# Chunk states of a Mamba-2 scan as three float32r passes on split operands, placed ahead of the samples' products

## The chip, the cores and the metric

The kernel runs on one core of one Trainium2 chip. The time is the device time of one execution in microseconds (us), start to end, weights and states read from the chip's main memory. Engines are named as the profile names them: PE is TensorE (its weight loads have a row kind of their own, PEld), DVE is VectorE, ACT is ScalarE, POOL is GpSimd, SP is SyncE, which here issues most DMAs. Each engine works its own instruction queue strictly in order; semaphores tie them together.

## What is computed

One inference step of a hybrid decoder layer for 256 prompt tokens and 8 samples of 8 tokens each (T = 320 columns). The part that matters is the chunked state-space scan of 8 groups of 8 heads. The prompt is cut in two chunks of 128 tokens. For each chunk the reference forms

```
to_end = jnp.exp(la_cs[:, :, -1:] - la_cs)
chunk_states = jnp.einsum('bcsgn,bcsgr,bcsgrp->bcgrpn', bm, to_end, xd)
```

that is, with B the 128 x 128 matrix of a chunk (tokens by state) and xw = xd * to_end its weighted inputs (128 tokens by 8 heads x 64), the product of B transposed and xw. The first chunk's state feeds the second chunk's output; both together make the prompt's final state. The samples start from states read from memory (`hin`), which are multiplied with C and then updated.

## The kernel before

Nearly all work is dense layers. `dense` and `dense2` take weights in units of 128 x 1024: SP loads a unit (`raw`), ACT rounds it to float32r (`wh`, L82), DVE makes the rest (`wl` = raw - wh, L83), and PE multiplies high by high, high by low and low by high (`mm3`, L88 to L90). `raw` has 4 buffers, `wh` and `wl` 3 each, so the unit n + 3 can be cast only when PE has done with unit n.

`mixer_ssd` runs groups g = 0 to 7. A group is a list of 18 jobs: for g < 7 six columns of the next group's input projection (`xbc`, jobs 0 to 5; each ends in a convolution of three DVE instructions L443 and a SiLU on ACT, L447), eight of the output projection of the group before (`ssm_out`), four gates. After job i the list `steps[i]` of `ssd` adds the scan's pieces: step 1 `by_token` (B transposed into `bt`, the masked product `cbm`), step 2 `x_by_token` (x transposed, `xd` = x dt on DVE, L528, `xw` = xd to_end on POOL, L530) and `sample_by_token`, step 4 `off_sample` twice (L617, eight products 32 columns wide, four side by side in PE) and `states` (L576, L579), step 5 `diagonal` (L594, whose results DVE adds with L596, called y), step 6 `off_prompt` (L605) and `off_sample_out` (transposes of `ye`, L201). The norm of the group before (`group_norm`: `ry`, L167 to L172, then L699 and splits L127, L128) comes after job 1. Group 0 has a shortened list and no norm; group 7 has `gate_pool` columns in place of the projection.

Tiles of one tag share buffers, and so does PSUM: the pool `misc` has 4 buffers handed out in turn, so each of these small products waits for the reader of the fourth before it. The framework orders the instructions of each engine ahead of time, by its own estimates; the order in the queues is fixed before the run.

Of the kernel before, what the change touches and what calls it, by code (L numbers as in the profile page):

```python
# [11 lines left out]
F32 = mybir.dt.float32  # L12
F32R = mybir.dt.float32r
AF = mybir.ActivationFunctionType
ALU = mybir.AluOpType
# [9 lines left out]
T = SEQ + NB * NS  # L25
# [28 lines left out]
def bcast(ap, shape):  # L54
    return ap.broadcast_to(list(shape))


class Kernel:
# [397 lines left out]
    def ssd(self, s, g):  # L456

        nc, I, O = self.nc, self.I, self.O
        h0 = 8 * g
        hs = slice(h0, h0 + 8)  # L460
        v = {"xd": [], "xw": [], "gt": [], "hin": {}}

        def heads(ap):
            return ap.rearrange("p (h d) -> p h d", h=8)
# [27 lines left out]
        def by_token():  # L492
            Bt, Ct = v["r"]["B"], v["r"]["C"]

            bt = v["bt"] = s.tile([128, 2, 128], F32, tag="bt", name="bt")
            ps = self.misc()
            for j in range(2):
                self.transpose(ps[:, j * 128:j * 128 + 128], Bt[:, j * 128:j * 128 + 128])
            self.transpose(ps[:64, 256:384], Bt[:, SEQ:T])
            nc.scalar.copy(out=bt.rearrange("p j n -> p (j n)"), in_=ps[:, :256])  # L500
            we = v["we"] = s.tile([128, 640], F32, tag="fin", name="we")[:64]
            nc.scalar.copy(out=we[:, 512:], in_=ps[:64, 256:384])

            cbm = s.tile([128, T], F32, tag="cbm", name="cbm")
            ps = self.misc()
            for j in range(2):
                js = slice(j * 128, j * 128 + 128)
                nc.tensor.matmul(ps[:, js], lhsT=Bt[:, js], rhs=Ct[:, js], start=True, stop=True)
            nc.tensor.matmul(ps[:64, 256:320], lhsT=Bt[:, SEQ:T], rhs=Ct[:, SEQ:T], start=True, stop=True)
            nc.vector.tensor_tensor(out=cbm[:, :SEQ].rearrange("p (j t) -> p j t", j=2),  # L510
                                    in0=ps[:, :SEQ].rearrange("p (j t) -> p j t", j=2),
                                    in1=bcast(self.cst[:, C_CM:C_CM + 128].unsqueeze(1), [128, 2, 128]), op=ALU.mult)
            nc.vector.tensor_tensor(out=cbm[:64, SEQ:], in0=ps[:64, 256:320], in1=self.cst[:64, C_SM:C_SM + 64], op=ALU.mult)

            for j, e in enumerate(v["gt"]):
                n = 128 if j < 2 else 64
                nc.vector.tensor_tensor(out=e[:n], in0=e[:n], in1=bcast(cbm[:n, j * 128:j * 128 + n].unsqueeze(1), [n, 8, n]),
                                        op=ALU.mult)

        def x_by_token():  # L520
            xs = v["r"]["x"]

            for j in range(2):
                ps = self.misc()
                for c in range(4):
                    self.transpose(ps[:, c * 128:c * 128 + 128], xs[:, c, j * 128:j * 128 + 128])
                d = s.tile([128, 512], F32, tag="xd", name="xd", bufs=2)
                nc.vector.tensor_tensor(out=heads(d), in0=heads(ps), in1=bcast(self.t_dt[:, j, hs].unsqueeze(2), [128, 8, 64]), op=ALU.mult)  # L528
                w = s.tile([128, 640], F32, tag="xw", name="xw", bufs=2)[:, :512]
                nc.gpsimd.tensor_tensor(out=heads(w), in0=heads(d), in1=bcast(self.t_end[:, j, hs].unsqueeze(2), [128, 8, 64]), op=ALU.mult)  # L530
                v["xd"].append(d)
                v["xw"].append(w)

        def sample_by_token():
            xs = v["r"]["x"]
# [17 lines left out]
        def rows_in(q):  # L553

            t = v["rw", q] = s.tile([128, 640], F32, tag="xw", name="rw", bufs=2)
            for j in range(4):
                o = 32 * q + 8 * j
                nc.sync.dma_start(out=t[32 * j:32 * j + 32], in_=bcast(
                    v["rows"][o:o + 8].rearrange("(o t) c -> o t c", o=1), [4, 8, 640]))
# [9 lines left out]
                                               in1=rw[:, w_], op0=ALU.mult, op1=ALU.add)  # L569

        def states():
            bt, xw = v["bt"], v["xw"]
            s0 = v["s0"] = s.tile([128, 512], F32, tag="s0", name="s0")
            fin = s.tile([128, 640], F32, tag="fin", name="fin")[:, :512]
            ps = self.misc()
            nc.tensor.matmul(ps, lhsT=bt[:, 0], rhs=xw[0], start=True, stop=True)  # L576
            nc.scalar.copy(out=s0, in_=ps)
            ps = self.misc()
            nc.tensor.matmul(ps, lhsT=bt[:, 1], rhs=xw[1], start=True, stop=True)  # L579
            nc.gpsimd.tensor_tensor(out=heads(fin), in0=heads(s0), in1=bcast(self.dec[:, hs, 1:2], [128, 8, 64]), op=ALU.mult)  # L580
            nc.vector.tensor_tensor(out=fin, in0=fin, in1=ps, op=ALU.add)
            nc.scalar.dma_start(out=O["ssm_prompt"][g], in_=fin)
# [29 lines left out]
        def off_sample(q):  # L612
            Ct = v["r"]["C"]
            pq = self.misc()
            for j in range(4):
                b = 4 * q + j
                nc.tensor.matmul(pq[32 * j:32 * j + 32, :], lhsT=Ct[:, SEQ + 8 * b:SEQ + 8 * b + 32],  # L617
                                 rhs=v["hin"][b // 2][:, b % 2, :], start=True, stop=True)
            ye = v["ye", q] = s.tile([128, 512], F32, tag="ye", name="ye", bufs=2)
            nc.scalar.copy(out=ye, in_=pq)  # L620
# [33 lines left out]
        def add_off():  # L654
# [8 lines left out]
        steps = {  # L663
            1: [by_token],
            2: [x_by_token, sample_by_token],
            4: [lambda: off_sample(0), lambda: off_sample(1), states],
            5: [diagonal, lambda: rows_in(0), lambda: rows_in(1)],
            6: [off_prompt, lambda: off_sample_out(0), lambda: off_sample_out(1)],
            7: [add_off],
# [21 lines left out]
    def group_norm(self, s, g, v):  # L691

        nc, y = self.nc, v["y"]
        r = s.tile([128, T], F32, tag="ry", name="ry")
        self.rstd(r, v["ssum"], self.ones_g, T)
        yh = s.tile([128, 4, T], F32R, tag="yh", name="yh")
        yl = s.tile([128, 4, T], F32R, tag="yl", name="yl")
        for c in range(4):
            nc.vector.scalar_tensor_tensor(out=y[:, c], in0=y[:, c], scalar=self.vec(V_SN + 4 * g + c), in1=r,  # L699
                                           op0=ALU.mult, op1=ALU.mult)  # L700
            self.split(yh[:, c], yl[:, c], y[:, c])
        v["yhl"] = (yh, yl)
# [567 lines left out]
```

## Time and profile before

| | |
|---|---|
| time, median of 3 runs | 2934.41 us (2933.08 to 2935.30) |
| profiled execution, its own time | 2932.04 us |
| its span in the trace | 2930.2 us |
| busy: PE, DVE, ACT, POOL | 2903.8, 1768.9, 1304.7, 454.4 us |
| granted clock of PE, mean | 0.998 of full speed (2.4 GHz) |

The span is the stretch from the first to the last instruction of the profiled execution; 1.84 us lie around it. Busy time of an engine counts its work, not its waits. A group of the scan repeats every 113.3 us; stamps below are us from the span's start, and the group looked at is g = 2.

### The profile page before, as it was taken

Reading aid. Unit: us, or ns where it says so; the run is one execution under the profiler, and the core shown is the slowest. Engines: PE = TensorE matmul, PEld = TensorE weight load, DVE = VectorE, ACT = ScalarE, POOL = GpSimd, SP = SyncE. Lnnn points to the kernel's source line nnn. Section 1 sums busy time; section 2 is a strip of 40 time slices with the busy share of each in tenths; the row PEclk is TensorE's granted clock in tenths of the full one; section 3 lists DMA queues with packets and bytes.
Section 4 is the critical chain, followed back from the end, with each engine's and each line's share of the span. In section 5 each row is a group of like instructions: output and inputs, shape, how many; then the busy total and the mean of one; then the engine's idle time right before and its main releaser. Section 6 shows DMA issues by size and latency. Waiting matters only on the chain.

```text
span 2930.2 us, 50017 instructions
## 1 busy us (share of the span) xinstructions
PE 2903.8 (99%) x20105; PEld 2821.0 (96%) x20105; DVE 1768.9 (60%) x2662; ACT 1304.7 (45%) x1866; POOL 454.4 (16%) x567
## 2 busy tenths in 40 slices
PE   9999999999999999999999999999999999999998
PEld 7999999999999999999999999999999999999997
DVE  5667576686776755554355555567666646645644
ACT  6535565455454444344333443345444434433434
POOL 3113132142231220231111100011000000000002
PEclk9999999999999999999999999999999999999999
DMA  7775655655645645544445477754444444444443
GB/s 280 245 229 190 228 188 171 222 159 197 225 154 202 225 151 186 181 154 164 152 171 187 151 252 281 262 184 154 151 154 149 155 151 151 151 153 148 153 151 115
DMA packets 173385, 536.93 MB, mean 183 GB/s; under 512 B 21344, under 2 KB 48224, under 8 KB 168928
## 3 DMA queue, kind: packets, MB, share of 16 engines
q1 hardware_dynamic: 162272, 515.14, 52.1%
q10 hardware_dynamic: 10880, 18.58, 1.8%
q8 instruction: 158, 2.59, 0.4%
q14 instruction: 75, 0.61, 0.1%
HBM read 497.09 MB, written 36.56 MB: 182 GB/s over the span
## 4 chain that ended last, share of the span: by engine, by line
PE 84%; DVE 8%; issue 2%; ACT 2%; DMA 2%; POOL 2%; SPq 0%; POOLq 0%; ACTq 0%; DVEq 0%
PE acc L88 27%; PE acc L89 26%; PE acc L90 26%; DVE wl L83 3%; DVE ca L443 1%; POOL hin L637 1%; ACT wh L82 1%; DVE g L488 1%; DMA raw<-in_w_ssm_out_dram 1%; DVE accs L711 1%; PE misc L981 1%; PE misc L943 1%; PE acc L239 0%; PE acc L240 0%; PE acc L238 0%
## 5 line engine op out<-in xcount | busy, mean ns | idle before, releaser
L83 DVE TENSOR_TENSOR wl<-raw,wh 128x1024 fp32r<-128x1024 f32 (+1 forms) x795 | 986.9, 1242 | 808.7 <-ACT wh L82 807.1
L82 ACT CAST wh<-raw 128x1024 fp32r<-128x1024 f32 (+1 forms) x795 | 829.9, 1045 | 1207.1 <-PE acc L89 830.4
L88 PE MATMUL acc<-a0h,wh 128*128 128x320 f32 (+1 forms) x2704 | 837.2, 310 | 0.0
L90 PE MATMUL acc<-a0h,wl 128*128 128x320 f32 (+1 forms) x2704 | 831.7, 308 | 1.3 <-DVE wl L83 1.3
L89 PE MATMUL acc<-a0l,wh 128*128 128x320 f32 (+1 forms) x2704 | 831.6, 308 | 0.0
L88 PE MATMUL acc<-a1h,wh 128*128 128x320 f32 x1920 | 592.1, 308 | 0.1
L89 PE MATMUL acc<-a1l,wh 128*128 128x320 f32 x1920 | 590.7, 308 | 0.0
L90 PE MATMUL acc<-a1h,wl 128*128 128x320 f32 x1920 | 590.5, 308 | 0.0
L88 PEld LDWEIGHTS acc<-a0h,wh 128*128 128x128 f32 (+1 forms) x2704 | 505.9, 187 | 3.5 <-ACT wh L82 1.6
L89 PEld LDWEIGHTS acc<-a0l,wh 128*128 128x128 f32 (+1 forms) x2704 | 505.9, 187 | 2.2 <-issue 1.9
L90 PEld LDWEIGHTS acc<-a0h,wl 128*128 128x128 f32 (+1 forms) x2704 | 505.9, 187 | 1.9 <-DVE wl L83 1.7
L88 PEld LDWEIGHTS acc<-a1h,wh 128*128 128x128 f32 x1920 | 359.8, 187 | 3.8 <-issue 2.8
L89 PEld LDWEIGHTS acc<-a1l,wh 128*128 128x128 f32 x1920 | 359.8, 187 | 1.8 <-issue 1.7
L90 PEld LDWEIGHTS acc<-a1h,wl 128*128 128x128 f32 x1920 | 359.8, 187 | 0.0
L154 POOL TENSOR_TENSOR ssum<-ssum,sq 128x320 f32<-128x320 f32 x63 | 64.6, 1025 | 893.3 <-ACT sq L153 892.8
L88 PE MATMUL acc<-yh,wh 128*128 128x320 f32 x512 | 161.3, 315 | 3.5 <-DVE accs L711 3.2
L89 PE MATMUL acc<-yl,wh 128*128 128x320 f32 x512 | 158.0, 309 | 0.0
L90 PE MATMUL acc<-yh,wl 128*128 128x320 f32 x512 | 157.9, 308 | 0.0
L443 DVE SCALAR_TENSOR_TENSOR ca<-ext,vecs,ca 128x344 f32<-128x344 f32 x144 | 108.0, 753 | 6.0 <-ACT ca L441 4.1
L88 PEld LDWEIGHTS acc<-yh,wh 128*128 128x128 f32 x512 | 96.0, 187 | 9.0 <-issue 8.0
L1075 DVE SCALAR_TENSOR_TENSOR fca<-fext,vecs,fca 128x336 f32<-128x336 f32 x176 | 99.5, 566 | 3.1
L1070 POOL COPY fnew<-fext 128x18 f32<-128x18 f32 x88 | 18.5, 210 | 528.3 <-DVE fext L1069 528.3
(295 smaller groups left out, 3679.8 us busy)
## 6 DMA issues: line engine op xcount, KB each, us to landing
raw<-in_w_up_dram SPq DMA_DIRECT2D x176, 512.0 KB
raw<-in_w_xbc_dram SPq DMA_DIRECT2D x96, 512.0 KB
raw<-in_w_down_dram SPq DMA_DIRECT2D x88, 512.0 KB
raw<-in_w_z_dram SPq DMA_DIRECT2D x64, 512.0 KB
raw<-in_w_ssm_out_dram SPq DMA_DIRECT2D x64, 512.0 KB
raw<-in_w_mem_k_dram SPq DMA_DIRECT2D x32, 512.0 KB
hin<-in_state_ssm_dram SPq DMA_DIRECT2D x32, 512.0 KB
raw<-in_w_gp_dram SPq DMA_DIRECT2D x32, 512.0 KB
```

Of the source, the lines that this page charges most:

```text
L82: nc.scalar.copy(out=wh[:, c], in_=raw[:, c])
L83: nc.vector.tensor_tensor(out=wl[:, c], in0=raw[:, c], in1=wh[:, c].bitcast(F32), op=ALU.subtract)
L88: nc.tensor.matmul(out, lhsT=wh, rhs=xh, start=first, stop=False)
L89: nc.tensor.matmul(out, lhsT=wh, rhs=xl, start=False, stop=False)
L90: nc.tensor.matmul(out, lhsT=wl, rhs=xh, start=False, stop=last)
L154: nc.gpsimd.tensor_tensor(out=ssum, in0=ssum, in1=sq, op=ALU.add)
L443: nc.vector.scalar_tensor_tensor(out=ca[:, 0:344], in0=e[:, j:j + 344], scalar=self.vec(V_CW + 48 * j + c), in1=ca[:, 0:344], op0=ALU.mult ...
L488: nc.vector.tensor_scalar(out=e[:n, h], in0=e[:n, h], scalar1=self.t_la[:n, j, h0 + h:h0 + h + 1], scalar2=0.0, op0=ALU.subtract, op1=ALU.min)
L637: nc.gpsimd.tensor_tensor(out=t.rearrange("p b (h d) -> p b h d", h=8), in0=t.rearrange("p b (h d) -> p b h d", h=8), in1=bcast(self.dec[: ...
L711: nc.vector.tensor_tensor(out=dst, in0=dst, in1=a, op=ALU.add)
L943: nc.tensor.matmul(ps[32 * b:32 * b + 32, :MEM], lhsT=qs[h % 2][:, dc, 4 * q + b], rhs=v["k", q][:, dc // 2, b, dc % 2], start=dc == 0, st ...
L1075: nc.vector.scalar_tensor_tensor(out=ca[:, :336], in0=e[:, j:j + 336], scalar=self.vec(V_FW + 88 * j + c), in1=ca[:, :336], op0=ALU.mult, ...
```

## The change

`bt` becomes a split pair (`bh`, `bl`). xw is made on DVE (new line L530) into an intermediate tile and split too: ACT casts `xwh`, DVE subtracts `xwl` (L128). `states` calls `mm3` twice: six float32r products in place of two float32 ones. Step 4 runs `states` ahead of the two `off_sample`. The tags change with it: the intermediate tiles take `s0` and `yo`, `xwh` takes `ye`, and the norm's `ry` takes the single buffer `cbm`, which `by_token` and the gates use.

```diff
-            bt = v["bt"] = s.tile([128, 2, 128], F32, tag="bt", name="bt")
+            bh, bl = v["bt"] = [s.tile([128, 256], F32R, tag=n_, name=n_) for n_ in ("bh", "bl")]
...
-            nc.scalar.copy(out=bt.rearrange("p j n -> p (j n)"), in_=ps[:, :256])
+            self.split(bh, bl, ps[:, :256])
...
-                w = s.tile([128, 640], F32, tag="xw", name="xw", bufs=2)[:, :512]
-                nc.gpsimd.tensor_tensor(out=heads(w), in0=heads(d), in1=bcast(self.t_end[:, j, hs].unsqueeze(2), [128, 8, 64]), op=ALU.mult)
+                w = s.tile([128, (512, 768)[j]], F32, tag=("s0", "yo")[j], name="xw")[:, :512]
+                nc.vector.tensor_tensor(out=heads(w), in0=heads(d), in1=bcast(self.t_end[:, j, hs].unsqueeze(2), [128, 8, 64]), op=ALU.mult)
+                wh = s.tile([128, 512], F32R, tag="ye", name="xwh", bufs=2)
+                wl = s.tile([128, 640], F32R, tag="xw", name="xwl", bufs=2)[:, :512]
+                self.split(wh, wl, w)
                 v["xd"].append(d)
-                v["xw"].append(w)
+                v["xw"].append((wh, wl))
...
-            ps = self.misc()
-            nc.tensor.matmul(ps, lhsT=bt[:, 0], rhs=xw[0], start=True, stop=True)
-            nc.scalar.copy(out=s0, in_=ps)
-            ps = self.misc()
-            nc.tensor.matmul(ps, lhsT=bt[:, 1], rhs=xw[1], start=True, stop=True)
+
+            def product(j):
+                ps = self.misc()
+                bh, bl = (b[:, j * 128:j * 128 + 128] for b in v["bt"])
+                self.mm3(ps, bh, bl, *v["xw"][j], True, True)
+                return ps
+
+            nc.scalar.copy(out=s0, in_=product(0))
+            ps = product(1)
...
-            4: [lambda: off_sample(0), lambda: off_sample(1), states],
+            4: [states, lambda: off_sample(0), lambda: off_sample(1)],
...
-        r = s.tile([128, T], F32, tag="ry", name="ry")
+        r = s.tile([128, T], F32, tag="cbm", name="ry")
```

The ready queues show where this lands. PE, step 4 of a middle group (1 to 7), before: `hin` and C are the samples' products, `xw` and `bt` the states.

```order
L90 MATMUL acc<-a0h,wl 128x320
L617 MATMUL misc<-hin,C 32x512 x8
L576 MATMUL misc<-xw,bt 128x512
L579 MATMUL misc<-xw,bt 128x512
L88 MATMUL acc<-a0h,wh 128x320
```

The same place of PE's queue now (L623 is the old L617):

```order
L90 MATMUL acc<-a0h,wl 128x320
L88 MATMUL misc<-xwh,bh 128x512
L89 MATMUL misc<-xwl,bh 128x512
L90 MATMUL misc<-xwh,bl 128x512
...
L88 MATMUL misc<-xwh,bh 128x512
L623 MATMUL misc<-hin,C 32x512 x5
L89 MATMUL misc<-xwl,bh 128x512
L90 MATMUL misc<-xwh,bl 128x512
L623 MATMUL misc<-hin,C 32x512 x3
L88 MATMUL acc<-a0h,wh 128x320
```

Six dense products stand where the dots are, and the second state is spread: its last two passes split the eight sample products into five and three. In group 0 the six passes and then the eight stand together.

DVE's queue before, from the norm to the end of step 1 (`cbm` and `g` are `by_token`, `newton` and `ry` the norm):

```order
L510 TENSOR_TENSOR cbm<-misc,cst 128x256
L513 TENSOR_TENSOR cbm<-misc,cst 64x64
L517 TENSOR_TENSOR g<-g,cbm 128x1024
L443 SCALAR_TENSOR_TENSOR ca<-ext_2130,vecs,ca 128x344
L167 TENSOR_TENSOR newton<-ry 128x320
```

The same two pieces of work now (L705 is the old L699):

```order
L167 TENSOR_TENSOR newton<-ry 128x320
...
L172 TENSOR_TENSOR ry<-ry,newton 128x320
L128 TENSOR_TENSOR bl<-misc,bh 128x256
L705 SCALAR_TENSOR_TENSOR y<-y,vecs,ry 128x320 x4
L83 TENSOR_TENSOR wl<-raw,wh 128x1024
L128 TENSOR_TENSOR yl<-y,yh 128x320 x4
L510 TENSOR_TENSOR cbm<-misc,cst 128x256
L513 TENSOR_TENSOR cbm<-misc,cst 64x64
L517 TENSOR_TENSOR g<-g,cbm 128x1024 x2
```

`by_token` has moved from ahead of the norm to behind all of it, since both now use one buffer. DVE's queue before, from step 2 to the final state `fin` (`xds` and `we` belong to the samples, `ext0` to `ext2` carry a number that tells the projection columns apart):

```order
L83 TENSOR_TENSOR wl<-raw,wh 128x1024
L539 TENSOR_TENSOR xds<-misc,t_dt 64x512
L548 TENSOR_TENSOR we<-misc,t_we 64x512
L443 SCALAR_TENSOR_TENSOR ca<-ext_2129,vecs,ca 128x344 x2
L83 TENSOR_TENSOR wl<-raw,wh 128x1024
L443 SCALAR_TENSOR_TENSOR ca<-ext_2129,vecs,ca 128x344
L83 TENSOR_TENSOR wl<-raw,wh 128x1024
L443 SCALAR_TENSOR_TENSOR ca<-ext_2130,vecs,ca 128x344 x3
L581 TENSOR_TENSOR fin<-fin,misc 128x512
```

The same place now:

```order
L128 TENSOR_TENSOR xwl<-xw,xwh 128x512
L530 TENSOR_TENSOR xw<-xd,t_end 128x512
L542 TENSOR_TENSOR xds<-misc,t_dt 64x512
L551 TENSOR_TENSOR we<-misc,t_we 64x512
L83 TENSOR_TENSOR wl<-raw,wh 128x1024
L128 TENSOR_TENSOR xwl<-xw,xwh 128x512
L443 SCALAR_TENSOR_TENSOR ca<-ext_2129,vecs,ca 128x344 x2
L443 SCALAR_TENSOR_TENSOR ca<-ext_2130,vecs,ca 128x344
L443 SCALAR_TENSOR_TENSOR ca<-ext_2129,vecs,ca 128x344
L443 SCALAR_TENSOR_TENSOR ca<-ext_2130,vecs,ca 128x344
L587 TENSOR_TENSOR fin<-fin,misc 128x512
L443 SCALAR_TENSOR_TENSOR ca<-ext_2130,vecs,ca 128x344
```

The second `xwl` stands behind one more unit's L83 than x_by_token did, and five convolution steps stand between it and `fin`, where three stood.

## Rows read from the trace of the kernel before

**Rows 1.** The page: busy times, and the costliest DVE group (busy us, mean ns)

```profile
PE 2903.8 (99%) x20105; PEld 2821.0 (96%) x20105; DVE 1768.9 (60%) x2662; ACT 1304.7 (45%) x1866; POOL 454.4 (16%) x567
L83 DVE TENSOR_TENSOR wl<-raw,wh 128x1024 fp32r<-128x1024 f32 (+1 forms) x795 | 986.9, 1242 | 808.7 <-ACT wh L82 807.1
```

**Rows 2.** Windows by stage: one middle group; length, then busy of PE, PEld, DVE, ACT, POOL

```profile
605.30:718.60 113.30, 111.71 (x789) 106.94 (x789) 82.08 (x132) 56.72 (x88) 32.96 (x25) 1.00 0.59 192
```

**Rows 3.** Waits, 378 to 1115 us: us in total, times, longest

```profile
PE misc L201 <- DVE y L596: 5.4, 12, 0.9
PEld misc L201 <- DVE y L596: 7.9, 12, 1.1
```

**Rows 4.** Timeline of PE: float32r products of 512 columns (start, duration us)

```profile
61.79 0.39 PE L238 MATMUL misc<-wh,mgh 128*128 128x512 f32 x1
62.03 0.39 PE L239 MATMUL misc<-wl,mgh 128*128 128x512 f32 x1
```

**Rows 5.** Timeline of PE, step 4 of group 2

```profile
618.70 1.92 PE L617 MATMUL misc<-hin,C 128*32 128x512 f32 x16
620.55 1.12 PE L576 MATMUL misc<-xw,bt 128*128 128x512 f32 x2
...
622.52 0.31 PE L89 MATMUL acc<-a0l,wh 128*128 128x320 f32 x1
622.67 0.31 PE L90 MATMUL acc<-a0h,wl 128*128 128x320 f32 x1
```

**Rows 6.** Timeline of DVE, group 2, steps 1 to 6

```profile
596.68 0.42 DVE L510 TENSOR_TENSOR cbm<-misc,cst 128x256 f32<-128x256 f32 x1
...
598.28 0.56 DVE L443 SCALAR_TENSOR_TENSOR ca<-ext,vecs,ca 128x344 f32<-128x344 f32 x1
600.09 0.49 DVE L167 TENSOR_TENSOR newton<-ry 128x320 f32<-128x320 f32 x1 [1.25 <-ACT ry L164]
...
612.69 0.67 DVE L528 TENSOR_TENSOR xd<-misc,t_dt 128x512 f32<-128x512 f32 x1
...
613.97 2.06 DVE L83 TENSOR_TENSOR wl<-raw,wh 128x1024 fp32r<-128x1024 f32 x1
...
619.37 0.57 DVE L443 SCALAR_TENSOR_TENSOR ca<-ext,vecs,ca 128x344 f32<-128x344 f32 x1
621.69 1.55 DVE L83 TENSOR_TENSOR wl<-raw,wh 128x1024 fp32r<-128x1024 f32 x1 [1.75 <-ACT wh L82]
623.16 4.92 DVE L443 SCALAR_TENSOR_TENSOR ca<-ext,vecs,ca 128x344 f32<-128x344 f32 x3
629.03 0.69 DVE L581 TENSOR_TENSOR fin<-fin,misc 128x512 f32<-128x512 f32 x1 [0.96 <-POOL fin L580]
...
633.60 1.02 DVE L568 SCALAR_TENSOR_TENSOR rw<-rh,cst,rw 128x512 fp32r<-128x512 f32 x2 [1.11 <-ACT rh L565]
...
636.62 0.54 DVE L596 SCALAR_TENSOR_TENSOR y<-x,vecs,misc 128x320 f32<-128x320 f32 x1
```

**Rows 7.** Timeline of POOL, group 2

```profile
610.82 4.13 POOL L530 TENSOR_TENSOR xw<-xd,t_end 128x512 f32<-128x512 f32 x2 [0.61 <-DVE xd L528]
...
620.23 1.93 POOL L637 TENSOR_TENSOR hin<-hin,dec 128x1024 f32<-128x1024 f32 x1
...
623.27 4.44 POOL L637 TENSOR_TENSOR hin<-hin,dec 128x1024 f32<-128x1024 f32 x2
627.67 1.33 POOL L580 TENSOR_TENSOR fin<-s,dec 128x512 f32<-128x512 f32 x1
```

**Rows 8.** Timeline of ACT: the cast behind fin's store, group 2; a gate behind its store, group 0

```profile
632.84 0.73 ACT L565 CAST rh<-rw 128x640 fp32r<-128x640 f32 x1 [1.61 <-DMA out_ssm_prompt_dram<-fin]
...
321.59 0.44 ACT L718 ACTIVATE gp<-acc 128x320 f32<-128x320 f32 x1 [2.31 <-DMA gp_dram<-gp]
```

**Rows 9.** Timeline of PE, steps 5 and 6 of group 2

```profile
629.50 0.66 PE L594 MATMUL misc<-g,xd 128*64 128x128 f32 x8
...
637.21 0.66 PE L201 MATMUL misc<-cst,ye 128*128 128x128 f32 x4 [0.67 <-DVE y L596]
638.16 0.66 PE L201 MATMUL misc<-cst,ye 128*128 128x128 f32 x4 [0.29 <-DVE y L596]
```

More of the change, by code (lines that the diff above doesn't have):

```diff
@@ L571, in states @@
         def states():
-            bt, xw = v["bt"], v["xw"]
             s0 = v["s0"] = s.tile([128, 512], F32, tag="s0", name="s0")
             fin = s.tile([128, 640], F32, tag="fin", name="fin")[:, :512]
-            ps = self.misc()
-            nc.tensor.matmul(ps, lhsT=bt[:, 0], rhs=xw[0], start=True, stop=True)
-            nc.scalar.copy(out=s0, in_=ps)
-            ps = self.misc()
-            nc.tensor.matmul(ps, lhsT=bt[:, 1], rhs=xw[1], start=True, stop=True)
+            def product(j):
[5 more added lines that the diff above has]
+            ps = product(1)
             nc.gpsimd.tensor_tensor(out=heads(fin), in0=heads(s0), in1=bcast(self.dec[:, hs, 1:2], [128, 8, 64]), op=ALU.mult)
```

## The prediction

> **What bounds the kernel now.** I read the page first: PE is busy 2903.8 of 2930.2 us, and its weight loads nearly as long [rows 1]. PE is the bound everywhere, so a change counts in two ways only: by the PE time that it adds or takes away, and by the places where PE waits for another engine. I then cut the scan into windows of one group [rows 2]. PE is busy 111.7 of 113.3 us there and DVE 82.1, so DVE has room over a group as a whole; what matters is when it is late within one. The waits show it: between 378 and 1115 us nearly all that PE waits for is L201 (the transposes of `ye` in step 6) behind L596 on DVE, 12 times, two in each of groups 1 to 6; counted at the weight loads it is 7.9 us, 1.3 us a group [rows 3]. L201 needs a `misc` buffer that L596 must have read. So in step 6 DVE already ends last, and whatever makes DVE later there costs PE time one for one.
>
> The timelines of group 2 show how DVE gets there. From L167 at 600.09 to the end of the convolution step at 619.94 it works without a gap; it then waits 1.75 us for a weight cast, and spends 4.92 us on three L443 that take some 0.57 us elsewhere [rows 6]. In these 4.92 us POOL multiplies two `hin` tiles, 4.44 us [rows 7]. Both engines' instructions read two operands from on-chip memory, and they take turns: one such DVE instruction goes through for each POOL instruction. DVE then waits for POOL's `fin` (L580), adds it (L581), a DMA stores it, ACT's L565 waits for that store because `rh` takes the buffer of `fin`, DVE's L568 waits for L565, and the y of L596 stand behind L568 [rows 6 to 8]. This chain from `fin` to the second L596 is 636.62 - 629.03 = 7.6 us long, and PE waits at its end [rows 9].
>
> **Term 1, PE's own work.** Before, step 4 takes from 618.70 to 622.37 (the L89 at 622.52 less one spacing of 0.15): the eight sample products 1.85 us, four side by side and so two rounds of 0.93; the two float32 products 1.82, or 0.91 each [rows 5]. A float32r product of this shape starts every 0.233 us [rows 4], so three take 0.70 and a group saves 2 x 0.21 = 0.42 us. But in groups 1 to 7 the queue cuts the eight sample products into five and three, with full-width passes between. That makes rounds of four, one and three: a third round, at most +0.93, and nothing if a single product could overlap the passes around it. No row shows a single one; a pass that takes all columns has no room beside it, so I take 0.93. Group 0 gets -0.4, groups 1 to 7 get +0.5 each (bounds -0.4 and +0.5).
>
> **Term 2, DVE's extra work, and whether the second state waits for it.** Added per group: two L530 and two `xwl` of 128 x 512, each like L528, 0.67 us [rows 6], of which some 0.07 overlap the neighbour (the L83 at 621.69 ends 0.08 after its successor starts [rows 6]); and `bl`, 256 wide, like L510, 0.42 less the same. Together 2.7 us. Taken away is POOL's work on xw, 4.13 us, which held DVE up: the L83 at 613.97 took 2.06 in place of 1.24, 0.8 us [rows 1, 6, 7]. And L510, L513 and the first L517, which filled 596.68 to 598.28 while the norm waited for ACT until 600.09 [rows 6], now follow the norm, since `ry` and `cbm` share a buffer: 1.6 us later.
>
> From 600.09 the old DVE queue had 19.85 us of work up to 619.94. The new queue up to the second `xwl` has that, less 0.8 (POOL), less three L443 that now come later (1.5), plus 1.6 (moved), 2.7 (added) and 1.15 (one more L83): 23.0 us, so `xwl` is ready at 623.1, and the first one, ahead of an L530, two sample instructions, an L83 and an `xwl`, 3.5 us earlier, at 619.6. PE comes to step 4 at 618.70 and wants the first `xwl` 0.23 later: a wait of 0.65. Then three passes, six dense ones (0.88), one pass, two rounds: it wants the second `xwl` at 622.9, a wait of 0.2. So PE leaves step 4 about 0.5 + 0.85 = 1.3 us later than before (bounds 0.5 and, if POOL's first `hin` product takes its turn just ahead of that `xwl`, 1.9 more [rows 7]). ACT gets two casts more, together as wide as one weight unit's; it is busy half of a group [rows 2] and makes them while it waits for DVE, and they cost nothing unless they hold up the cast of a weight unit, which PE wants two units later, 7 us (24 passes of 0.15 us a unit [rows 5]).
>
> **Term 3, the chain from `fin`.** Five L443 now stand ahead of `fin` in place of three. Started at 623.1 and at 4.92 / 3 = 1.64 each, they end at 631.3, and `fin` starts 2.3 us later than at 629.03. If they ran at 0.5 us, POOL's own `fin` would hold it at about 629, no change; if each of them and the `xwl` lost a whole POOL product, it would be 4.5. I take 2.2, nearest to the row of the same instructions beside the same POOL work. The chain behind `fin` is shorter by the narrow L571, now behind the first y (-0.3). So the second y comes 2.0 us later than before. PE meets this twice: the second `misc` buffer of step 5 is now that of the second state, which `fin` frees at 632.0, while PE reaches step 5 at 629.50 + 1.3 [rows 9] and the second product 0.55 later, a wait of 0.6; and at L201, where it arrives 1.9 later than before and waits as before. Either way PE leaves step 6 when DVE lets it: +2.0 us a group.
>
> **Term 4, the rest.** Group 7 has no L443, and no L201 wait before; it gets the +0.5 of term 1. The last norm must now wait for the store of a `gp` tile in its buffer; a wait of this kind took 2.31 us [rows 8], but ACT casts a unit meanwhile and two gate columns lie ahead of the reader: I take 0.2 (0 to 2). Weight units, SP's loads (the rows that SP fetches wait for `xwl` now, a microsecond later, with four raw buffers ahead) and the norm's other steps are hidden by 7 us or more of dense products; without that cover each would show as PE waiting for L83.
>
> **The sum.** Six groups at +2.0 are 12.0; group 0 -0.4; group 7 +0.5; the end +0.2: +12.3 us. Of the profiled execution's 2932.04 that makes 2944.3. Its time lay 2.4 below the median of 2934.41, so the forecast as a median is 2946.7, say 2947, 0.4% slower. No change here means within 0.2%, 5.9 us, which is about what a measurement of this kernel can tell.
>
> **The rivals.**
> *DVE keeps up* (no change). The L443 run without POOL in their way, or the 0.96 us in which DVE waits for POOL at `fin` [rows 6] and the 1.75 before it soak up the extra work. Then only term 1 and a part of the waits are left: 0 to +0.9 a group, about +3 us, 2937. For it speaks that POOL's `fin` is now third in its queue and was fourth; against it that the same L443 were slow in this very place.
> *The products win* (faster). A lone sample product costs nothing extra and `fin` comes earlier by one `hin` product, so that the 1.3 us of waiting at L201 vanish. A group then saves 0.4 + 1.3, less the first wait for `xwl`: 8 to 11 us in all, about 2925. It decides if the second y is ready before PE's new arrival, 1.3 us later than at L201 now; DVE would have to be no later than today with 2.7 us more to do.
> *Turns with POOL* (much slower). Each of DVE's two-operand instructions from 622 to 633 waits out a whole POOL instruction of 1.3 to 1.9 us, `xwl` among them, so that PE waits in step 4 too and `fin` starts 4.5 us late: six times 4.5, +27 us, 2962. The rows show such turns, but not for single instructions. The Trainium skill says of this (SBUF — State Buffer, section Who interferes with whom) that a VectorE instruction with two inputs in SBUF contends with a GpSimd instruction that reads SBUF, and that the loser is blocked for the other's whole instruction and isn't merely throttled. By that rule this rival would be the forecast, 2962; the trace agrees in kind, 4.92 us for three L443 beside two `hin` products.
> *The split doesn't do what it says* is no rival here: the queues show the six passes.
>
> **How the numbers follow.** The forecast's case gets 0.52 (own range 2941 to 2956, +1.2 to +3.5 a group), keeping up 0.27, turns 0.13, faster 0.08. Slower is the first and the third, 0.65; the same 0.27; faster 0.08. The range takes in the bounds of the terms: 2932, at which groups gain nothing and half the waits vanish, to 2963, the case of turns.
>
> **What would show it.** In the changed profile: L88 to L90 on `misc` with 512 columns 0.23 us apart, and L623 in three rounds; PE waiting for `xwl` in step 4 by under a microsecond; `fin` on DVE starting 12 to 13 us after PE enters step 4 (10.3 now); waits of PE for L587 or L602 of 2 us or more a group. The forecast is wrong if L443 ahead of `fin` take their 0.57 us, or if PE does not wait for L602 any more.

## The result, and the profile after

The change makes the kernel slower: 2949.17 us (median of 4 runs, 2948.27 to 2951.56) against 2934.14 (4 runs, 2933.08 to 2935.30), a ratio of 1.0056 with a 95% interval of 1.0044 to 1.0068. The forecast was 2947. The profiled execution took 2948.27 us, its span is 2946.4: 16.2 more than before, where 12.3 had been summed up.

One correction to the text ahead: the group whose step 4 starts at 618.70, called group 2 there, is the fourth, g = 3. It is called the group of the rows here; in the changed kernel its step 4 starts at 622.12.

First the page's busy line, which answers to [rows 1], then a window of one group (length, busy PE, PEld, DVE, ACT, POOL), which answers to [rows 2].

```profile
PE 2913.0 (99%) x20121; PEld 2822.9 (96%) x20121; DVE 1803.2 (61%) x2702; ACT 1312.1 (45%) x1881; POOL 419.9 (14%) x551
```

```profile
506.58:622.12 115.54, 113.12 (x792) 107.26 (x790) 87.01 (x137) 57.64 (x89) 25.15 (x23) 1.00 0.60 189
```

PE is still busy 99% of the span. This group is 2.24 us longer than in [rows 2]; PE's busy time has grown by 1.41 of them, the rest is waiting (over the whole run busy time grew by 9.2 of 16.2 us). PE's waits between 360 and 1130 us (total, times, longest), which answer to [rows 3]:

```profile
PE misc L201 <- DVE y L602: 6.9, 12, 0.9
PE misc L600 <- DVE fin L587: 4.7, 6, 0.8
```

The wait at L201 stays, as forecast, and a new one has come, for `fin`, once in each of groups 1 to 6. Together they are 11.6 us where 5.4 were, 1.0 us a group more. PE's timeline of step 4 to step 6 in the group of the rows, against [rows 5] and [rows 9]:

```profile
622.12 0.39 PE L88 MATMUL misc<-xwh,bh 128*128 128x512 f32 x1
622.47 0.50 PE L89 MATMUL misc<-xwl,bh 128*128 128x512 f32 x1
622.80 0.39 PE L90 MATMUL misc<-xwh,bl 128*128 128x512 f32 x1
623.03 0.31 PE L88 MATMUL acc<-a0h,wh 128*128 128x320 f32 x1
...
623.90 0.39 PE L88 MATMUL misc<-xwh,bh 128*128 128x512 f32 x1
624.22 1.90 PE L623 MATMUL misc<-hin,C 128*32 128x512 f32 x10
626.05 0.50 PE L89 MATMUL misc<-xwl,bh 128*128 128x512 f32 x1
626.39 0.40 PE L90 MATMUL misc<-xwh,bl 128*128 128x512 f32 x1
626.72 1.06 PE L623 MATMUL misc<-hin,C 128*32 128x512 f32 x6
627.71 0.42 PE L88 MATMUL acc<-a0h,wh 128*128 128x320 f32 x1
627.96 0.31 PE L89 MATMUL acc<-a0l,wh 128*128 128x320 f32 x1
...
636.74 0.66 PE L600 MATMUL misc<-g,xd 128*64 128x128 f32 x8 [0.80 <-DVE fin L587]
```

The eight sample products take 1.83 (624.22 to 626.05) and 0.99 (626.72 to 627.71) in place of one 1.85: three rounds. The passes of the states start 0.23 apart only where nothing changes beside them, and 0.32 to 0.35 beside the sample products or where `xwl` is just late. From 622.12 to 627.81 (the L89 at 627.96 less 0.15), less the six dense passes between (0.87), step 4 takes 4.82 us; it was 3.67.

DVE and POOL in the same group, against [rows 6] and [rows 7]:

```profile
603.25 0.49 DVE L167 TENSOR_TENSOR newton<-ry 128x320 f32<-128x320 f32 x1 [1.28 <-ACT ry L164]
...
611.73 0.41 DVE L510 TENSOR_TENSOR cbm<-misc,cst 128x256 f32<-128x256 f32 x1
...
625.27 0.67 DVE L128 TENSOR_TENSOR xwl<-xw,xwh 128x512 fp32r<-128x512 f32 x1
625.87 10.22 DVE L443 SCALAR_TENSOR_TENSOR ca<-ext,vecs,ca 128x344 f32<-128x344 f32 x5
636.01 0.68 DVE L587 TENSOR_TENSOR fin<-fin,misc 128x512 f32<-128x512 f32 x1
...
642.86 0.54 DVE L602 SCALAR_TENSOR_TENSOR y<-x,vecs,misc 128x320 f32<-128x320 f32 x1
```

```profile
625.37 2.37 POOL L643 TENSOR_TENSOR hin<-hin,dec 128x1024 f32<-128x1024 f32 x1 [2.28 <-PE misc L623]
627.69 0.49 POOL L438 COPY cnew<-ext 128x27 f32<-128x27 f32 x1
628.15 1.94 POOL L643 TENSOR_TENSOR hin<-hin,dec 128x1024 f32<-128x1024 f32 x1
630.04 1.34 POOL L586 TENSOR_TENSOR fin<-s,dec 128x512 f32<-128x512 f32 x1
631.34 4.38 POOL L643 TENSOR_TENSOR hin<-hin,dec 128x1024 f32<-128x1024 f32 x2
```

Five L443 take 10.22 us, and POOL works through five two-operand instructions and a small copy in just that time (625.37 to 635.72): one DVE instruction for each long one of POOL. Taken one by one in the trace, the five end at 628.11, 630.45, 631.75, 633.92 and 636.09, each 0.37 or 0.38 us after one of POOL's five ends. So the turns that the prediction had from sums alone can be seen instruction by instruction. `fin` starts 13.9 us after PE enters step 4; it was 10.3. The Trainium skill (SBUF — State Buffer, Who interferes with whom) says that a DVE instruction with two inputs in SBUF contends with a POOL instruction that reads SBUF, and that the one which issues second is blocked until the other is through; the trace agrees, 2.04 us an L443 in place of 0.57.

Where the 16.2 us lie, read off the starts of PE's instructions:

| stretch | us more than before |
|---|---|
| up to step 4 of group 0 | +0.4 |
| group 0 and up to step 4 of group 1 | -1.75 |
| groups 1 to 6, start of step 4 to end of step 6 | +2.0 to +2.8 each, 15.0 in all |
| the same groups, the rest | -0.1 in all |
| group 7, start of step 4 to end of step 6 | +1.1 |
| from there to the end | +1.4 |

### The profile page after: what moved, and what is told of

Same layout as the page of the kernel before. It is cut to its first block, busy times and chain, and to the rows that moved or that the text cites. A ratio compares the mean times of both kernels' runs of the same rounds, so it can differ in the third digit from the quotient of the medians.

```text
span 2946.4 us, 50107 instructions
## 1 busy us (share of the span) xinstructions
PE 2913.0 (99%) x20121; PEld 2822.9 (96%) x20121; DVE 1803.2 (61%) x2702; ACT 1312.1 (45%) x1881; POOL 419.9 (14%) x551
## 4 chain that ended last, share of the span: by engine, by line
PE 87%; DVE 7%; ACT 2%; DMA 2%; issue 2%; POOL 0%; ACTq 0%; SPq 0%; POOLq 0%; DVEq 0%
PE acc L88 27%; PE acc L89 27%; PE acc L90 27%; DVE ca L443 2%; DVE wl L83 2%; DMA g<-la_dram 1%; ACT wh L82 1%; PE misc L201 1%; DVE accs L717 1%; PE misc L987 1%; PE misc L949 1%; DMA raw<-in_w_ssm_out_dram 0%; PE acc L239 0%; PE acc L240 0%; DVE g L488 0%
## 5 line engine op out<-in xcount | busy, mean ns | idle before, releaser
L83 DVE TENSOR_TENSOR wl<-raw,wh 128x1024 fp32r<-128x1024 f32 (+1 forms) x795 | 981.9, 1236 | 790.1 <-ACT wh L82 789.8
L82 ACT CAST wh<-raw 128x1024 fp32r<-128x1024 f32 (+1 forms) x795 | 829.4, 1045 | 1208.1 <-PE acc L89 829.3
L89 PE MATMUL acc<-a0l,wh 128*128 128x320 f32 (+1 forms) x2704 | 831.8, 308 | 0.0
L89 PE MATMUL acc<-a1l,wh 128*128 128x320 f32 x1920 | 590.7, 308 | 0.0
L89 PEld LDWEIGHTS acc<-a0l,wh 128*128 128x128 f32 (+1 forms) x2704 | 506.0, 187 | 0.5
L89 PEld LDWEIGHTS acc<-a1l,wh 128*128 128x128 f32 x1920 | 359.8, 187 | 1.8 <-issue 1.7
L89 PE MATMUL acc<-yl,wh 128*128 128x320 f32 x512 | 158.1, 309 | 1.1 <-DVE yl L128 1.1
L443 DVE SCALAR_TENSOR_TENSOR ca<-ext,vecs,ca 128x344 f32<-128x344 f32 x144 | 129.1, 908 | 13.2 <-ACT ca L441 11.8
L90 PE MATMUL acc<-fh,wl 128*128 128x320 f32 x320 | 98.7, 308 | 0.0
```

What stands on the lines that cost most here:

```text
L82: nc.scalar.copy(out=wh[:, c], in_=raw[:, c])
L83: nc.vector.tensor_tensor(out=wl[:, c], in0=raw[:, c], in1=wh[:, c].bitcast(F32), op=ALU.subtract)
L89: nc.tensor.matmul(out, lhsT=wh, rhs=xl, start=False, stop=False)
L90: nc.tensor.matmul(out, lhsT=wl, rhs=xh, start=False, stop=last)
L443: nc.vector.scalar_tensor_tensor(out=ca[:, 0:344], in0=e[:, j:j + 344], scalar=self.vec(V_CW + 48 * j + c), in1=ca[:, 0:344], op0=ALU.mult ...
```

## The experiments

All were timed beside the kernel before; the ratio is to its time on the same chip. Three stage times are means over groups 1 to 6, taken from the starts of instructions in the timelines: when `fin` starts and when step 6 ends, both counted from PE's entry into step 4, and the period of a group (a fifth of the way from step 4 of group 1 to that of group 6).

| kernel | ratio (95%) | fin | step 6 ends | period |
|---|---|---|---|---|
| before | 1 | 10.3 | 19.8 | 113.3 |
| changed | 1.0056 (1.0044 to 1.0068) | 13.9 | 22.3 | 115.7 |
| e1 changed, hin in halves | 1.0021 (1.0012 to 1.0030) | 10.4 | 20.9 | 114.5 |
| e2 changed, no hin | 0.9995 (0.9986 to 1.0004) | 7.7 | 20.0 | 113.2 |
| e3 before, no hin | 0.9965 (0.9952 to 0.9979) | 6.75 | 18.8 | 112.1 |
| e4 changed, old order of step 4 | 1.0080 (1.0067 to 1.0093) | 13.9 | 22.6 | 116.1 |
| e5 before, ry in cbm | 1.0067 (1.0054 to 1.0079) | 13.5 | 22.7 | 116.1 |
| e6 before, xw on DVE | 1.0041 (1.0029 to 1.0054) | 12.3 | 21.2 | 115.35 |
| e7 before, hin in halves | 1.0007 (0.9998 to 1.0016) | 10.7 | 20.0 | 113.6 |
| e8 changed, mended | 1.0018 (1.0009 to 1.0026) | 10.3 | 19.9 | 114.7 |
| e9 changed, ry in s0 | 1.0036 (1.0023 to 1.0049) | 10.2 | 19.9 | 115.5 |
| e10 before, hin late | 1.0147 (1.0133 to 1.0160) | 6.75 | 19.0 | 119.8 |
| e11 changed, mended, hin late | 1.0118 (1.0103 to 1.0134) | 6.1 | 18.2 | 118.4 |
| e12 changed, halves, eight together | 1.0048 (1.0034 to 1.0062) | 13.5 | 22.3 | 115.85 |

**e1, the length of a turn.**

```diff
-                nc.gpsimd.tensor_tensor(
-                    out=t.rearrange("p b (h d) -> p b h d", h=8), in0=t.rearrange("p b (h d) -> p b h d", h=8),
-                    in1=bcast(self.dec[:, hs, 2 + b:4 + b].rearrange("p h b -> p b h").unsqueeze(3), [128, 2, 8, 64]), op=ALU.mult)
+                for k in range(2):
+                    nc.gpsimd.tensor_tensor(out=heads(t[:, k]), in0=heads(t[:, k]),
+                                            in1=bcast(self.dec[:, hs, 2 + b + k:3 + b + k], [128, 8, 64]), op=ALU.mult)
```

> The changed kernel with each of POOL's hin multiplications (1024 columns) cut into two of 512; all other queues keep their order. Theory (turns): each of the five L443 ahead of fin lets one whole POOL instruction go first, so their 10.22 us in group 2 follow the length of POOL's instructions. With halves they take about 5.5 to 7 us, fin starts about 10 us after PE enters step 4 in place of 13.9, PE's waits behind fin and y shrink by some 2 us a group, and the time is about 2936 (2932 to 2940). Rival (shared bytes): DVE and POOL share a rate, so halves change nothing: 10 us, 2949. Rival (PE's own work): fin comes earlier but PE's third round of sample products costs the time, and 2946 to 2949 stays.

DVE's L443 ahead of `fin`, in the group of the rows:

```profile
623.00 6.70 DVE L443 SCALAR_TENSOR_TENSOR ca<-ext,vecs,ca 128x344 f32<-128x344 f32 x5
```

Five take 6.70 us, 1.34 each: the turn follows the length of POOL's instruction. `fin` comes 3.5 us earlier, step 6 ends 1.4 earlier, and the ratio falls from 1.0056 to 1.0021. The turns are shown, and a rate that the engines share is ruled out: POOL moves the same bytes.

**e2 and e3, no multiplication at all.** Both kernels leave out the multiplication in `update`.

```diff
-            for i in (2 * q, 2 * q + 1):
-                t, b = v["hin"][i], 2 * i
-                nc.gpsimd.tensor_tensor(
...
```

> The changed kernel without POOL's multiplication of the samples' states by their decay (left out; the states get only the new part added). Theory (turns): L443 take 0.56 us each, fin starts within 10 us of PE entering step 4, PE no longer waits for fin or y; what stays is PE's own 1.15 us a group: about 2934 (2930 to 2937). Rival (DVE's extra instructions make it late by themselves): fin still 12 us or later, time within 3 us of 2949.

> The kernel before, also without that multiplication (left out). Theory: its 1.3 us a group of waits behind y vanish, about 2926 (2924 to 2929); the changed kernel without it is then still 6 to 10 us slower than this, which is PE's own part of the loss. Rival (PE's own work costs nothing, everything is the turns): the two without multiplication are within 3 us of each other.

2930.89 and 2921.46 us: 9.4 apart, where the full kernels are 15 apart. The five L443 ahead of `fin` take 2.64 us in e2. Without turns, what the change costs is PE's step 4 (its own work and some 0.2 of waiting for `xwl`): step 5 starts 11.96 after step 4 in one and 10.80 in the other, 1.16 more, and the period grows by as much, 113.24 against 112.09. So 9.4 of the 15 us stay without the multiplication, and the rest comes with it. The kernel before itself pays 11 us for the multiplication, more than was expected: 2921.46 lies below the range of e3.

**e4, the old order of step 4.**

```diff
-            4: [states, lambda: off_sample(0), lambda: off_sample(1)],
+            4: [lambda: off_sample(0), lambda: off_sample(1), states],
```

> The changed kernel with the samples' products in front of the states again, so that the eight stand together; DVE's queue in groups 1 to 6 is the same. PE saves the third round and the switches, about 1.15 us in step 4. Theory (DVE's chain from fin ends last): PE then waits that much longer in steps 5 and 6, groups 1 to 6 gain under 0.5 us each, group 7 gains 1: 2945 to 2949. Rival (PE's own work adds up): seven groups gain 1.15 each, about 2941.

PE's waits between 360 and 1130 us:

```profile
PE misc L600 <- DVE fin L587: 10.9, 6, 1.8
PE misc L201 <- DVE y L602: 3.5, 6, 0.9
```

PE gets its microsecond back (step 5 starts 10.9 after step 4, not 12.0) and spends it waiting for `fin` a microsecond longer (1.8 in place of 0.8). Step 6 ends no earlier in groups 1 to 6. Group 7, which has no L443, gains 1.3. That bears out the theory; the time, 2955.6, missed both figures, because group 0 lost 7 us, told in the last section.

**e5, the shared buffer alone**, and **e6, xw on DVE alone**, each in the kernel before, with PE's queue unchanged:

```diff
-        r = s.tile([128, T], F32, tag="ry", name="ry")
+        r = s.tile([128, T], F32, tag="cbm", name="ry")
```

```diff
-                nc.gpsimd.tensor_tensor(out=heads(w), in0=heads(d), in1=bcast(self.t_end[:, j, hs].unsqueeze(2), [128, 8, 64]), op=ALU.mult)
+                nc.vector.tensor_tensor(out=heads(w), in0=heads(d), in1=bcast(self.t_end[:, j, hs].unsqueeze(2), [128, 8, 64]), op=ALU.mult)
```

> The kernel before with one edit: the norm's ry takes the buffer of cbm. PE's queue is the same; on DVE L510, L513 and a first L517 move behind the norm, 1.6 us. Theory: DVE's two waits ahead of fin (1.75 for a weight cast and 0.96 for POOL) soak this up, and what is left is the last norm's wait for a gp store, about 1.3: 2932 to 2937, as a guess 2934. Rival (every DVE delay ahead of fin reaches PE): six groups at 1.6, 2942.

> The kernel before with one edit: xw is multiplied on DVE in place of POOL. PE's queue is the same. DVE gets two instructions of 0.6 us and gets back 0.8 at the L83 that POOL held up: +0.4 us, soaked up by the waits ahead of fin: within 3 us of before. Rival (DVE's load decides): up to six times 1.2, +7.

Both theories fell, and the times lie above the rivals' figures too. e5 alone is slower than the whole change. DVE in its group of the rows (step 4 at 624.77):

```profile
606.16 0.49 DVE L167 TENSOR_TENSOR newton<-ry 128x320 f32<-128x320 f32 x1 [1.27 <-ACT ry L164]
...
614.44 0.42 DVE L510 TENSOR_TENSOR cbm<-misc,cst 128x256 f32<-128x256 f32 x1
...
625.83 5.24 DVE L443 SCALAR_TENSOR_TENSOR ca<-ext,vecs,ca 128x344 f32<-128x344 f32 x3
...
633.23 5.16 DVE L443 SCALAR_TENSOR_TENSOR ca<-ext,vecs,ca 128x344 f32<-128x344 f32 x3 [1.02 <-ACT ca L441]
638.31 0.68 DVE L581 TENSOR_TENSOR fin<-fin,misc 128x512 f32<-128x512 f32 x1
```

The 1.6 us of L510, L513 and L517 moved out of DVE's idle time ahead of the norm push a second set of three L443 into the stretch in which POOL multiplies. Six run at 1.7 us where three did, and 1.6 us of delay become 3.2 at `fin`. In e6 the cause is on the other engine. POOL no longer makes xw, and in its new queue all four `hin` stand ahead of `fin` (the last two and `fin` are shown); DVE waits for POOL's `fin`:

```profile
630.25 4.11 POOL L637 TENSOR_TENSOR hin<-hin,dec 128x1024 f32<-128x1024 f32 x2
634.32 1.06 POOL L580 TENSOR_TENSOR fin<-s,dec 128x512 f32<-128x512 f32 x1
```

```profile
635.41 0.69 DVE L581 TENSOR_TENSOR fin<-fin,misc 128x512 f32<-128x512 f32 x1 [2.85 <-POOL fin L580]
```

So `fin` starts at the later of two things: the end of DVE's L443, and POOL's `fin`, which stands behind some number of `hin` products in POOL's queue (two in the changed kernel, three before, four in e6).

**e7, halves in the kernel before**, with e1's edit.

> The kernel before with POOL's hin multiplications in halves. Theory (turns): three L443 take some 3 us in place of 4.92, fin starts 1 us or more earlier, and most of PE's 1.3 us a group of waiting for y goes: 2926 (2922 to 2930), against 2921.5 without the multiplication at all. Rival (POOL's halves only add fixed cost): no gain, 2932 to 2936.

The L443 got faster (3.15 us for three, was 4.92 in [rows 6]) but `fin` stands behind six halves on POOL and starts at 10.7. No gain: the theory named only one of the two things.

**e12, halves and the eight together**: e1's edit, and `states` cut in two.

```diff
-            4: [states, lambda: off_sample(0), lambda: off_sample(1)],
+            4: [state0, lambda: off_sample(0), lambda: off_sample(1), state1],
```

> The changed kernel with hin in halves, and with the first state ahead of the samples' products and the second behind them, so that the eight stand together; ry stays in cbm's buffer. Theory (in a group the later of PE's own work and DVE's chain counts): with the halves DVE's chain ends 1 us or less after PE, so of the 1.15 us that PE gets back in step 4 about half counts in groups 1 to 6 and all of it in group 7: 4 us below the kernel with halves alone, a ratio to the kernel before of about 1.0008 (0.9998 to 1.0015). Rival (DVE's chain always ends last): no gain but group 7's, a ratio of 1.0017 to 1.0025.

Slower than e1 and above both expected ratios, and again through POOL's queue. DVE, then POOL, in its group of the rows:

```profile
624.12 5.75 DVE L443 SCALAR_TENSOR_TENSOR ca<-ext,vecs,ca 128x344 f32<-128x344 f32 x5
633.87 0.69 DVE L589 TENSOR_TENSOR fin<-fin,misc 128x512 f32<-128x512 f32 x1 [4.01 <-POOL fin L588]
```

```profile
622.51 5.20 POOL L646 TENSOR_TENSOR hin<-hin,dec 128x512 f32<-128x512 f32 x3 [1.17 <-PE misc L625]
...
628.11 4.71 POOL L646 TENSOR_TENSOR hin<-hin,dec 128x512 f32<-128x512 f32 x4
632.78 1.05 POOL L588 TENSOR_TENSOR fin<-s,dec 128x512 f32<-128x512 f32 x1
```

With the second state behind the samples' products, seven halves are queued ahead of `fin` where e1 had four. The L443 are done at 629.87, and DVE idles 4.01.

**e9, the shared buffer undone** in the changed kernel, and **e8**, which adds e1's and e12's edits:

```diff
-        r = s.tile([128, T], F32, tag="cbm", name="ry")
+        r = s.tile([128, 512], F32, tag="s0", name="ry")[:, :T]
```

> The changed kernel with one edit: ry takes the buffer of s0 in place of cbm's, so that L510, L513 and a first L517 come ahead of the norm again, in DVE's idle time. Theory (the shared buffer makes DVE late): fin starts 1.5 to 3 us earlier than 13.9 after PE enters step 4, PE's waits behind fin go, and groups 1 to 6 gain 1 to 2 us each: 2940 (2935 to 2944); the last norm's wait of 1.1 us goes too. Rival (the split's instructions on DVE make it late, the buffer matters only in the kernel before): fin within 1 us of 13.9, time within 3 us of the changed kernel.

> The changed kernel mended in three places: the first state ahead of the samples' products and the second behind them (the eight stand together), POOL's hin multiplications in halves, and ry in the buffer of s0 in place of cbm's. Theory: step 4 costs PE 1.0 us less than in the changed kernel, the 1.6 us on DVE come back, the turns are half as long: 2938.7 with halves alone becomes 2931 (2927 to 2935), and the last norm's wait of 1.1 goes. Rival (DVE's added instructions still end last): 2936 or more.

e9 brings `fin` back to 10.2, and PE waits neither for `fin` nor for y. Yet the period is 115.5, nearly the changed kernel's: step 6 ends 2.4 earlier and the rest of the group is 2.2 longer. PE's waits between 240 and 1130 us, and ACT in the group of the rows:

```profile
PE acc L88 <- DVE accs L717: 6.7, 5, 1.8
PE acc L88 <- ACT wh L82: 5.3, 5, 1.1
```

```profile
644.64 0.73 ACT L568 CAST rh<-rw 128x640 fp32r<-128x640 f32 x1 [6.04 <-DMA rw<-rows]
...
645.92 1.99 ACT L82 CAST wh<-raw 128x1024 fp32r<-128x1024 f32 x2
```

The second `rh` now waits 6.04 us for its rows (2.51 in the kernel before), and two weight casts stand behind it. Those rows come by eight loads. The first six are issued 4.1 to 7.6 us after PE enters step 4, earlier than in the kernel before (5.0 to 8.4), so it is not the later `we` that holds them. The last two stand in SP's queue behind a weight load, which goes out as soon as the L83 behind `fin` has ended. DVE's L83 and POOL beside it, then the same L83 in the kernel before:

```profile
635.12 2.66 DVE L83 TENSOR_TENSOR wl<-raw,wh 128x1024 fp32r<-128x1024 f32 x1 [1.49 <-ACT wh L82]
632.88 3.83 POOL L643 TENSOR_TENSOR hin<-hin,dec 128x1024 f32<-128x1024 f32 x2
```

```profile
631.26 1.23 DVE L83 TENSOR_TENSOR wl<-raw,wh 128x1024 fp32r<-128x1024 f32 x1 [1.54 <-ACT wh L82]
```

This L83 meets POOL's last `hin` and ends 15.1 us after PE enters step 4, where it was 13.8; the last two loads go out 1.3 later by the same measure. It is one more turn, in a new place. The rows then take another 1.3 longer to arrive; the runs do not show why. Of the 4.5 us gained overall, 1.4 are group 7's and 1.1 the last norm's wait, which is gone. e8 has a step 4 shorter than before (step 5 starts 10.56 after it, was 10.80) and a `fin` as early as before, and pays in the same later places: PE waits 4.2 us for `accs` and 4.3 for casts. Its time is the rival's. 1.0018 is the best that a split version with all its work got, within the noise of e1's 1.0021.

**e10, the multiplication behind step 6** in the kernel before, and **e11**, the same in e8's kernel without the halves: the four products come after `add_off` and read a copy of the decays whose tile shares the buffer of `el`.

```diff
+        def scale_states():
+            k = v["dk"] = s.tile([128, 4, 192], F32, tag="el", name="dk")
+            k = k[:, 0, :64].rearrange("p (h b) -> p h b", h=8)
+            nc.gpsimd.tensor_copy(out=k, in_=self.dec[:, hs, 2:10])
...
-            7: [add_off],
+            7: [add_off, scale_states],
```

> The kernel before with POOL's four hin multiplications moved behind y's last addition (they read a copy of the decays that shares a buffer with el, so that they start when step 6 is over). Theory: the L443 ahead of fin run at 0.57 us as without the multiplication, fin starts 6 to 8 us after PE enters step 4 in place of 10.3, PE's 1.3 us a group of waits behind y go: 2924 (2921 to 2929). Rival (the turns only move): DVE's L83 and accs additions behind step 6 take turns instead, PE waits for acc or wl there: 2931 or more.

> The split states with all the mends: first state ahead of the samples' products and second behind them, ry in the buffer of s0, hin multiplied behind step 6. Theory: PE's step 4 is 0.2 us shorter than in the kernel before, no turns ahead of fin, and the added DVE instructions fit: 2921 to 2928. Rival (DVE's 2.7 us a group still end last somewhere): 3 or more above the kernel before with the same late multiplication.

e10 is far slower, in the way that its rival said but by much more. e11 comes out 10 us below e10, so both its figures missed: the theory's, and the rival's, which put it above e10. In both, `fin` is as early as without the multiplication, but DVE meets the turns in the next stretch. POOL, DVE, and PE's waits of e10:

```profile
664.49 7.60 POOL L638 TENSOR_TENSOR hin<-hin,dk 128x1024 f32<-128x1024 f32 x4
```

```profile
664.63 7.93 DVE L488 TENSOR_SCALAR g<-g,t_la 128x128 f32<-128x128 f32 x6
672.49 0.47 DVE L716 TENSOR_TENSOR accs<-accs,acc 128x320 f32<-128x320 f32 x1
672.88 0.67 DVE L488 TENSOR_SCALAR g<-g,t_la 128x128 f32<-128x128 f32 x3
```

```profile
PE acc L88 <- DVE accs L716: 30.0, 5, 6.0
```

Of the six small L488 that take 7.93 us together, four take 1.88 to 1.97 each, one for each of POOL's four instructions (1.9 each); the other two are as short as the three behind them, 0.22 apart. `accs` behind them frees PE's accumulator, and PE waits up to 6.0 us. The waits are not the whole price: around this one PE's granted clock was 0.81, 0.50 and 0.84 in the windows from 668 to 680 us (4 us each), and its mean over the run is 0.990, where it was 0.998.

## Why the prediction was right, and where its sum was off

The sign and the mechanism were right: DVE is late in the chain from `xwl` over L443 and `fin` to y, PE waits at the end of it in groups 1 to 6, and these groups make up 15.0 of 16.2 us. Of the signs that it named, three rounds and a short wait for `xwl` came as said; `fin` came 13.9 us after PE's entry into step 4, not 12 to 13, and PE's waits behind L587 and L602 are 1.9 us a group, just under the 2 named. That 2947 lies so near the median is in part luck: some of its errors cancelled. By its steps:

**Term 1** was mis-sized: +0.5 a group was forecast. The third round added 0.97 (1.83 and 0.99 against 1.85), where 0.93 was taken. What was missed is the change between full-width passes and products 32 columns wide, about 0.1 us each of four times. Passes, rounds and changes together cost 0.95 a group. The Trainium skill (TensorEngine Tiling (Array Packing), Key Properties) says that changing the tiling mode drains the engine; the trace agrees in that each change costs time (0.32 to 0.34 in place of 0.23), but it does not show a drain as such.

**Term 2**: PE was to leave step 4 1.3 us later, 0.85 of it from waiting; it left 1.15 later, with only some 0.2 of waiting for `xwl`. The errors of terms 1 and 2 cancelled, which was luck. Where nothing hid it, this was the cost: group 7 +1.14 against +0.5, and e2 against e3.

**Term 3** was mis-sized where it was least sure. L443 took 2.04 us, not 1.64, and `fin` started 3.6 us later against step 4, not 2.3. Behind it the chain was shorter than supposed (6.85 us from `fin` to the second y; 7.6 before, 7.3 taken), and the groups lost 2.5 rather than 2.0. The wait at step 5's product was 0.8 for 0.6. The rival *turns with POOL* had the mechanism more exactly: each L443 lost a whole instruction of POOL's. But `xwl` did not, and its 27 us were not reached.

**Term 4**: in the last norm ACT waited 0.43 us for a `gp` store, PE waited 1.1 behind it for `yl`, and the end came 1.4 later, where 0.2 was taken out of 0 to 2; with `ry` in another buffer (e9) that wait of PE is gone. Group 0 gained 1.75 up to group 1, where 0.4 was forecast; a wait of 1.30 of PE for L83 at 306.98 in the kernel before isn't there any more, and step 4 is 0.3 shorter.

**The method** failed in one place that the time hides. The working added up delays in DVE's queue, as if a microsecond moved were a microsecond late. e5 and e6 show otherwise: the buffer alone makes 1.0067 and xw on DVE alone 1.0041, both together with the split 1.0056. The same addition led to wrong expectations for e5, e6, e8 and e9. One reading ahead hid where the gain would go: L201 was called nearly all that PE waits for between 378 and 1115 us, but beside its 5.4 us that view has 3.2 us of waits for `accs`, in five groups. There e8 to e11 pay. What decides is the later of two queues, and how many instructions fall into POOL's stretch. What part each edit has in the 15 us can therefore not be told as a sum. Nor was a version found that does all the work and beats the kernel before: e7 is level with it.

## What to carry to other kernels

Two engines that take turns make a delay grow: count which instructions a delay pushes into the other engine's stretch, not only its length, and look where the result stands in the other engine's queue. A buffer saved by sharing is paid for where the work that it holds back stood in idle time; price it by a run of that edit alone. Work that PE gets back is worth nothing in a stage whose end another engine sets.

## What the runs showed of the hardware

A small instruction pays the turn as a large one does: in e10 an L488 of 128 columns, 0.22 us where POOL is idle, took 1.9 beside each of POOL's 1.9 us instructions. And a longer wait of PE can cost more than its length. In e4 PE waited 1.93 us for a cast (L82) and 1.14 for an L83 around 306 to 310, in group 0; why they came late there is not shown. Windows of e4 (length, busy PE, PEld, DVE, ACT, POOL, then the granted clock), then of the kernel before, where PE waited 1.30 at that place:

```profile
308.00:312.00 4.00, 2.86 (x11) 2.59 (x12) 1.71 (x5) 3.96 (x6) 1.62 (x1) 0.57 0.35 105
312.00:316.00 4.00, 4.00 (x19) 3.62 (x17) 1.74 (x2) 3.85 (x5) 0.00 (x0) 0.58 0.30 71
```

```profile
308.00:312.00 4.00, 4.00 (x27) 3.37 (x27) 1.23 (x1) 3.96 (x6) 0.00 (x0) 1.00 0.33 129
```

The granted clock fell to 0.57 for 8 us, most of them at the lower of its two levels (1.2 GHz): 19 products in 4 us in place of 27. Group 0 of e4 up to step 4 of group 1 took 7.3 us longer than in the changed kernel, some 3 of it waits, which is why e4's time missed both expectations. In e10 the clock fell in the same way around all five waits of 6.0 us: 0.50 to 0.54 in a 4 us window at the end of each.
